# A fused two-block kernel: 32-row tap tables, a new order at the start of the second block, and a gated delta rule with its side products and norm re-cut

## The chip, the cores and the metric

One core of one Trainium2 chip runs the whole program. The metric is device time of one execution in microseconds (us). TensorE (PE), VectorE (DVE), ScalarE (ACT), GpSimd (POOL) and SyncE (SP) each have their own queue of instructions and wait for each other by semaphores; in this kernel SP issues nearly all loads.

## What is computed

256 tokens of width 1024, batch 1, all in float32. A first block of one layer, then a second block of two layers:

```python
def hybrid_mixer(xn, ...):
    b_gate, c_gate, h_conv, qkv, z, beta_logit, a_logit = split(xn @ w_in)
    y_conv = b_gate * causal_depthwise_conv(c_gate * h_conv, conv_w)      # 3 taps
    q, k, v = split(silu(causal_depthwise_conv(qkv, dn_conv_w)))          # 4 heads of 128
    o = chunk_gated_delta_rule(l2norm(q), l2norm(k), v, g, beta)          # chunks of 64
    y_dn = rms_norm(o, dn_norm) * silu(z)
    return concat([y_conv, y_dn]) @ w_out
def chunk_gated_delta_rule(...):
    t_mat = inverse(1 + strict_lower(k_beta k^T * decay))                 # per chunk
    u, w = t_mat @ v_beta, t_mat @ (k_beta * exp(g))
    intra = (q k^T) * decay
    for each chunk:                                                       # the scan
        v_new = u - w @ state
        o = (q * exp(g)) @ state + intra @ v_new
        state = state * exp(g_last) + k_dec^T @ v_new
first block:  h += hybrid_mixer;  h += cross_attention(mem);  h += peer_ffn;  x = rms_norm(h)
second block: x += gate * conv_mixer(x)   # 31-tap depthwise convolution, layer norm
              x += gate * pool_mixer(x)   # window means of 2, 4, 8, 16
```

`peer_ffn` takes the 16 best of 16384 experts for each of 8 heads of each token.

## The kernel before

Activations lie transposed: channels on the partitions, 256 tokens along the free dimension. Weights come as tiles of 128x1024 float32 (512 KB), each loaded by SP into a buffer `raw` (L113). ACT rounds a tile to the matmul's fp32r format (`hi`, L142), DVE (POOL for some) subtracts (`lo`, L144), and PE runs 24 matmuls of 128x256 on it: `hi` with the upper part of the activation, `hi` with its lower part, `lo` with the upper part (L155 to L157, L186 to L188, L1263 to L1265). Before the tiles in `plan` come in one fixed order, through rings of three buffers, so a load starts when a buffer comes free and a tile is split when its turn comes.

All other work is written as generators (`spawn`), which `tick` moves on between the tiles: evacuations of PSUM, convolutions, norms, the chain of the delta rule. Each engine's queue is then ordered by the framework's own timeline scheduler, within the priorities that the code gives (`urgent`, `high_priority`, `issue_after`). An engine runs its queue strictly in order.

The places that the change touches:

- **The mixer (L496 to L531).** In this order: the projections of k, two of four blocks of the attention's memory values (`values(0, 1)`), q, v, `values(2, 3)`, z, four pairs of `ch_evac` (convolution branch, `cp` and `ycv`, L693 to L698), two pairs of the b gate (`b_evac`, L703); then `residual` with `w_out`, whose matmuls L186 to L188 read the mixer's output `xb`: `b_evac` writes its first half (L289 and L297 split it), the delta rule its second.
- **The delta rule (`delta`, L737 to L927).** Per block of 128 tokens (two), it builds the chunk inverse by five levels of small f32 matmuls (L790, L797, L802), one step per tick. After all levels come `kbg` and `kdec` (L822, L824), and then, when q and v are there, `vb` (L833), `w`, `u`, the masked product `it` (L849) and two zero-padded copies of decayed q (`qd`, L855; POOL clears their other halves). The scan has four chunk steps: `pws` (L877), `E` = u minus it (L878, the new values), `pd` (L884), the state `S` (L891 for each head; L887 in the first). The output `po` (L900, L902) is copied by ACT. At the end the norm runs per pair of heads over all tokens: square `sqo` (L910), `on` (L912), `ov` (L914), Ln, Exp, one Newton step (L244 to L246), a POOL multiply by silu(z), then L926 and the split L289, L290.
- **Loads for the second block (`second_prep`, L1331 to L1365).** During the second half of `peer_down` (L1236 to L1266) a generator has SP load `rcnt`, `fwd`, the tap tables `ftap` (31x512) and `dw` (31x1024), and later `inv`, between the weight tiles.
- **The start of the second block (`second`, L1396).** `first_out` (L1287) makes the last sums `s` (L1298). From `s` follow `v` (L1408), `rho` (L1410, L1411, Newton) and the input `xah`, `xal` (`mod_input`, L1386, L1387) for the first matmul `mmv` (L212). The taps' transform is eight matmuls of `dw` and `ftap` (`wfm`, `wfp`, L1422) with a copy each on ACT (L1423), and `x0_gen` takes a column sum `cs` (L268) and rescales `h`.

Of the kernel before, what the change touches and what calls it, by code (L numbers as in the profile page):

```python
# [6 lines left out]
F32 = mybir.dt.float32  # L7
# [33 lines left out]
class Net:  # L41
# [26 lines left out]
    def plan(self):  # L68
# [428 lines left out]
    def mixer(self):  # L497
# [29 lines left out]
        for p in range(2):  # L527
            b = self.pair(xa, lambda ps, p=p: self.b_evac(ps, p))
# [207 lines left out]

    def delta(self):  # L737
# [69 lines left out]
        up_y(0)  # L807
        yield
        for li in range(1, nl):
            up_te(0, li)  # L810
            up_y(1)
            yield
            if li < nl - 1:
                up_y(0)
            up_te(1, li)
            yield
        for tb in range(2):
# [6 lines left out]
            V.tensor_mul(kdec[tb], pk, bc(self.ed[:, tb, :]))  # L824
            yield
        yield from self.wait("q0", "q1", "v0", "v1")
        us, wTs, inT, qds = [], [], [], []
        for tb in range(2):
            pv = pst("pv")
            for hh in R4:  # L830
                P.transpose(pv[:, hh, :], vT[:, hh, TS[tb]], ident)
            vb = t512(f"am{tb}")
            V.tensor_mul(vb, pv, bc(self.beta[:, tb, :]))  # L833
# [12 lines left out]
            for hh in R4:
                P.matmul(pq[:, hh, :], lhsT=kT[:, hh, TS[tb]], rhs=qT[:, hh, TS[tb]], start=True, stop=True)
            it = t512(f"A{tb}")
            V.tensor_mul(it, pq, self.decT[tb])  # L849
            qd = []  # L850
            for c in range(2):
                x = t512(f"kbg{tb}" if c else f"dA{tb}")
                G.memset(x[:, :, 64 * (1 - c):64 * (2 - c)], 0.0)
# [961 lines left out]
```

## Time and profile before

| what | value |
|---|---|
| median of 3 runs | 1341.28 us (1340.36 to 1341.85) |
| the profiled execution | 1340.44 us |
| its span in the trace | 1338.2 us |
| mean granted clock of TensorE | 0.987 of full speed |
| busy: PE, DVE, ACT, POOL | 1291.0, 988.9, 643.1, 168.0 us |
| loads | 236.88 MB, 178 GB/s over the span |

The span is the part of the execution that the trace covers; 2.2 us lie around it. PE is busy for 96% of the span, so 47 us of the span are left in which it does nothing, and a granted clock under 1 tells that part of its busy time ran at the lower of two levels.

### The profile page before, as it was taken

The numbers are of one execution on the slowest core, as the hardware profiler recorded it, in microseconds if no ns is written. First come the engines' busy times: TensorE is split into PE (matmuls) and PEld (weight loads), VectorE is DVE, ScalarE is ACT, GpSimd is POOL, SyncE is SP. The second block draws the span as 40 slices with busy tenths as digits, with TensorE's granted clock in tenths as the row PEclk, the third lists the DMA queues.
The fourth block names the chain that finished last, engine by engine and source line by source line (L and its number), as shares of the span: only waits on it lengthen the run. The fifth ranks groups of instructions, "written<-read, shape, count | busy, mean of one in ns | idle before, by whom it ended". The sixth has DMA issues, their size and how long they took to land.

```text
span 1338.2 us, 27259 instructions
## 1 busy us (share of the span) xinstructions
PE 1291.0 (96%) x11212; PEld 1262.5 (94%) x11212; DVE 988.9 (74%) x1885; ACT 643.1 (48%) x841; POOL 168.0 (13%) x175
## 2 busy tenths in 40 slices
PE   7999988999999999999999999998999998998988
PEld 7999978989999999999999999997999996998987
DVE  7897756458488837888878999985666666677884
ACT  6674335445554544343444344444444445356652
POOL 0000000002728362000000000010100000000000
PEclk9999998999999999999999999998999998998999
DMA  7644324434566667666677766676777772433553
GB/s 241 198 143 139 90 85 136 147 116 153 174 190 179 198 181 231 214 204 212 200 222 214 215 199 210 205 238 184 234 235 236 235 221 71 137 120 103 183 166 107
DMA packets 67340, 239.69 MB, mean 179 GB/s; under 512 B 8146, under 2 KB 8402, under 8 KB 67088
## 3 DMA queue, kind: packets, MB, share of 16 engines
q1 hardware_dynamic: 59536, 212.79, 52.7%
q0 software_dynamic: 7680, 25.17, 5.7%
q8 instruction: 87, 1.43, 0.4%
q14 instruction: 37, 0.30, 0.1%
HBM read 236.88 MB, written 1.05 MB: 178 GB/s over the span
## 4 chain that ended last, share of the span: by engine, by line
PE 90%; DVE 4%; ACT 2%; DMA 2%; issue 1%; SPq 0%; DVEq 0%; ACTq 0%
PE mm L155 14%; PE mm L157 14%; PE mm L156 14%; PE y L1263 9%; PE y L1265 9%; PE y L1264 9%; DVE lo L144 2%; PE mmv L212 2%; PE mm L187 2%; PE mmv L214 2%; PE mmv L213 2%; PE mm L188 2%; PE mm L186 2%; PE G L1215 1%; PE G L1216 1%; DMA raw<-in_V 1%
## 5 line engine op out<-in xcount | busy, mean ns | idle before, releaser
L142 ACT ACTIVATE hi<-raw 128x1024 fp32r<-128x1024 f32 x391 | 412.7, 1060 | 554.8 <-PE mm L156 229.0
L144 DVE TENSOR_TENSOR lo<-raw,hi 128x1024 fp32r<-128x1024 f32 x347 | 423.8, 1224 | 184.0 <-ACT hi L142 182.8
L155 PE MATMUL mm<-xbh,hi 128*128 128x256 f32 x1128 | 319.4, 283 | 0.3 <-ACT hi L142 0.3
L157 PE MATMUL mm<-xbh,lo 128*128 128x256 f32 x1128 | 316.8, 281 | 1.0 <-DVE lo L144 0.8
L156 PE MATMUL mm<-xbl,hi 128*128 128x256 f32 x1128 | 316.1, 280 | 0.0
L1263 PE MATMUL y<-xbh,hi 128*128 128x256 f32 x1008 | 285.1, 283 | 5.0 <-ACT hi L142 5.0
L1264 PE MATMUL y<-xbl,hi 128*128 128x256 f32 x1008 | 284.3, 282 | 0.0
L1265 PE MATMUL y<-xbh,lo 128*128 128x256 f32 x1008 | 283.8, 282 | 0.5 <-DVE lo L144 0.5
L157 PEld LDWEIGHTS mm<-xbh,lo 128*128 128x128 f32 x1128 | 212.2, 188 | 1.6 <-DVE lo L144 1.6
L155 PEld LDWEIGHTS mm<-xbh,hi 128*128 128x128 f32 x1128 | 212.6, 188 | 0.6 <-ACT hi L142 0.5
L156 PEld LDWEIGHTS mm<-xbl,hi 128*128 128x128 f32 x1128 | 212.6, 189 | 0.1
L1263 PEld LDWEIGHTS y<-xbh,hi 128*128 128x128 f32 x1008 | 190.9, 190 | 5.2 <-ACT hi L142 5.2
L1265 PEld LDWEIGHTS y<-xbh,lo 128*128 128x128 f32 x1008 | 190.6, 189 | 1.5 <-DVE xbl L297 0.8
L1264 PEld LDWEIGHTS y<-xbl,hi 128*128 128x128 f32 x1008 | 191.2, 190 | 0.0
L155 PE MATMUL mm<-xah,hi 128*128 128x256 f32 x448 | 128.2, 287 | 3.1 <-ACT xah L1386 3.1
L144 POOL TENSOR_TENSOR lo<-raw,hi 128x1024 fp32r<-128x1024 f32 x44 | 106.1, 2413 | 199.4 <-DVE mt L1094 123.5
L156 PE MATMUL mm<-xal,hi 128*128 128x256 f32 x448 | 128.5, 287 | 0.7 <-DVE xal L1387 0.7
L157 PE MATMUL mm<-xah,lo 128*128 128x256 f32 x448 | 128.2, 287 | 0.5 <-DVE lo L144 0.5
L1323 POOL DMA_DIRECT2D wm<-in_w_mod x96 | 51.7, 539 | 528.2 <-DVE wm L1326 512.3
L155 PEld LDWEIGHTS mm<-xah,hi 128*128 128x128 f32 x448 | 84.9, 190 | 4.3 <-ACT xah L1386 3.3
L1326 DVE SCALAR_TENSOR_TENSOR wm<-wm,silu_c 128x512 f32<-128x512 f32 x96 | 68.9, 718 | 25.0 <-DMA wm<-in_w_mod 24.6
L156 PEld LDWEIGHTS mm<-xal,hi 128*128 128x128 f32 x448 | 85.0, 190 | 2.0 <-DVE xal L1387 0.9
(463 smaller groups left out, 2181.1 us busy)
## 6 DMA issues: line engine op xcount, KB each, us to landing
raw<-in_U SPq DMA_DIRECT2D x128, 512.0 KB, 3.7
raw<-in_V SPq DMA_DIRECT2D x128, 512.0 KB, 4.2
wm<-in_w_mod POOLq DMA_DIRECT2D x96, 256.0 KB, 4.0
raw<-in_w_in SPq DMA_DIRECT2D x28, 512.0 KB, 3.7
raw<-in_cv_ab SPq DMA_DIRECT2D x16, 512.0 KB, 3.7
raw<-in_pl_in SPq DMA_DIRECT2D x16, 512.0 KB, 4.0
raw<-in_w_xk SPq DMA_DIRECT2D x8, 512.0 KB, 4.8
raw<-in_w_xv SPq DMA_DIRECT2D x8, 512.0 KB, 4.2
```

Of the source, the lines that this page charges most:

```text
L142: self.A.activation(hi, raw, AF.Copy)
L144: i = (self.G if self.order[m][1] else self.V).tensor_sub(lo, raw, hi.bitcast(F32))
L155: self.P.matmul(ps, lhsT=hi[:, w], rhs=xh[:, k, :], start=(k == 0 and first), stop=False, skip_group_check=True)
L156: self.P.matmul(ps, lhsT=hi[:, w], rhs=xl[:, k, :], start=False, stop=False, skip_group_check=True)
L157: self.last_mm = self.P.matmul(ps, lhsT=lo[:, w], rhs=xh[:, k, :], start=False, stop=(k == KB - 1), skip_group_check=True)
L186: self.P.matmul(o, lhsT=hi[:, c], rhs=xh[:, k, :], start=a, stop=False, skip_group_check=True)
L187: self.P.matmul(o, lhsT=hi[:, c], rhs=xl[:, k, :], start=False, stop=False, skip_group_check=True)
L1263: P.matmul(o, lhsT=hi[:, w], rhs=wh[:, s, :], start=(j == 0 and db % 2 == 0), stop=False, skip_group_check=True)
L1264: P.matmul(o, lhsT=hi[:, w], rhs=wl[:, s, :], start=False, stop=False, skip_group_check=True)
L1265: P.matmul(o, lhsT=lo[:, w], rhs=wh[:, s, :], start=False, stop=(j == 127), skip_group_check=True)
L1323: nc.gpsimd.dma_start(w, self.I["w_mod"][n, :, 512 * c:512 * (c + 1)])
L1326: V.scalar_tensor_tensor(w, w, 1.0, s, op0=OP.mult, op1=OP.mult, accum_out=part[:, n, c:c + 1])
```

## The change

Three parts. (1) `ftap` and `dw` get 32 rows, the last of zeros. (2) At the start of the second block the chain to `rho` and `mod_input` has high priority, the taps' matmuls after the first two wait for the last `s`, their copies for the Exp of `rho`, and the rescaling of `h` for the end of `mod_input`. (3) In the mixer all four `values` stand behind k. `keys` (for `kbg`, `kdec`) runs inside levels 2 and 3; a new generator `sides` makes `vb`, `it` and `qd` when the levels are done, beside `delta`; `qd` is no longer padded, its matmuls cover 64 columns. The norm runs per block of 128 tokens (`norm`), squares straight from PSUM, and takes silu(z) and the gain in one DVE operation. The last two pairs of tiles (the b gate) are not started until the scan has been issued, and stand behind the last `po` on PE.

```diff
 CW = 31
+CP = 32
...
-        add([I["w_xv"][b] for b in range(4)], "V")
-        add([w[b] for b in (*range(12, 16), *range(20, 24))], "V")
-        add([I["w_xv"][b] for b in range(4, 8)], "V")
-        add([w[b] for b in range(24, 28)], "V")
+        add([I["w_xv"][b] for b in range(8)], "V")
+        add([w[b] for b in (*range(12, 16), *range(20, 28))], "V")
...
-                self.values(0, 1)
+                self.values(0, 1, 2, 3)
             if nm == "q":
                 self.spawn(self.qsum())
-        self.values(2, 3)
+            if nm == "v":
+                self.spawn(self.urgent(self.sides()))
...
-        for p in range(2):
-            b = self.pair(xa, lambda ps, p=p: self.b_evac(ps, p))
+        while "scan" not in self.flags:
+            self.tick()
+        with self.tc.issue_after(self.last_po.ins):
+            for p in range(2):
+                b = self.pair(xa, lambda ps, p=p: self.b_evac(ps, p))
...
+    def sides(self):
...
+        yield from self.wait("v0", "v1", "levels")
+        self.vb = []
...
+            pv = self.psT.tile([128, 4, 128], F32, tag="t", name="pv")
+            for hh in range(4):
+                P.transpose(pv[:, hh, :], vT[:, hh, ts], self.ident)
+            vb = mix.tile([128, 4, 128], F32, tag="S", bufs=2, name="vb")
+            V.tensor_mul(vb, pv, self.beta[:, tb, :].unsqueeze(2).to_broadcast([128, 4, 128]))
+            self.vb.append(vb)
+        self.flags.add("vb")
...
+            pq = self.psT.tile([128, 4, 128], F32, tag="t", name="pq")
...
+            it = mix.tile([128, 4, 128], F32, tag=f"A{tb}", name="it")
+            V.tensor_mul(it, pq, self.decT[tb])
+            qd = mix.tile([128, 4, 128], F32, tag=f"dA{tb}", name="qd")
+            V.tensor_mul(qd, qT[:, :, ts], self.egr[tb])
+            self.inT.append(it)
+            self.qd.append(qd)
+        self.flags.add("it")
...
+        up_y(0)
+        yield
+        for li in range(1, nl):
+            up_te(0, li)
+            up_y(1)
+            if li in (2, 3):
+                keys(li - 2)
+            yield
+            if li < nl - 1:
+                up_y(0)
+            up_te(1, li)
+            yield
+        self.flags.add("levels")
...
+        yield from self.wait("vb")
...
+        yield from self.wait("it", "z0", "z1", "qv")
...
+        def norm(tb, po):
+            o, v, r, q = oT[:, :, TS[tb]], t512(f"yy{tb}"), t512(f"T{tb}"), t512(f"am{tb}")
+            A.activation(q, po, AF.Square)
+            V.scalar_tensor_tensor(o, po, self.col("dn_norm", 0), self.zs[:, :, TS[tb]], op0=OP.mult, op1=OP.mult)
+            yield
+            ps = pst("on")
+            P.matmul(ps, lhsT=self.ones, rhs=q, start=True, stop=True)
+            V.scalar_tensor_tensor(v, ps, 1.0 / 128, self.qv[:, :, TS[tb]], op0=OP.mult, op1=OP.add)
+            A.activation(r, v, AF.Ln)
...
+            V.tensor_mul(o, o, r)
+            V.scalar_tensor_tensor(q, q, -1.0, v, op0=OP.mult, op1=OP.mult)
+            V.scalar_tensor_tensor(o, q, 1.5, o, op0=OP.add, op1=OP.mult)
...
+            x = [t[:, 4:8, TS[tb]] for t in self.xb]
+            A.activation(x[0], o, AF.Copy)
+            V.tensor_sub(x[1], o, x[0].bitcast(F32))
...
-                yield
...
-                if c == 0:
-                    yield
...
-                        P.matmul(po[:, hh, :], lhsT=before[c][:, hh, :], rhs=qds[tb][c][:, hh, :], start=first, stop=False)
+                        cs = slice(64 * c, 64 * c + 64)
+                        P.matmul(po[:, hh, cs], lhsT=before[c][:, hh, :], rhs=self.qd[tb][:, hh, cs], start=first,
+                                 stop=False, skip_group_check=True)
                         first = False
-                P.matmul(po[:, hh, :], lhsT=vn[:, hh, :], rhs=inT[tb][:, hh, :], start=first, stop=True)
-            A.activation(oT[:, :, TS[tb]], po, AF.Copy)
-            yield
...
-            G.tensor_mul(o, o, self.zs[:, 2 * p:2 * p + 2, :])
...
+                self.last_po = P.matmul(po[:, hh, :], lhsT=vn[:, hh, :], rhs=self.inT[tb][:, hh, :], start=first,
+                                        stop=True, skip_group_check=True)
+            n = norm(tb, po)
+            next(n)
+            if tb == 0:
+                n0 = n
+            else:
+                for _ in n0:
+                    pass
+                for _ in n:
+                    pass
+                self.flags.add("scan")
...
-        self.ftap = pool.tile([CW, 4, 128], F32, name="ftap")
+        self.ftap = pool.tile([CP, 4, 128], F32, name="ftap")
         nc.sync.dma_start(self.ftap, I["ftap"])
-        self.dw = pool.tile([CW, D], F32, name="dw")
...
-        V.tensor_scalar(v2, s2, EPS * EPS, None, op0=OP.add)
         rho = post.tile([128, T], F32, name="rho")
-        A.activation(rho, v2, AF.Ln)
-        A.activation(rho, rho, AF.Exp, scale=-0.5)
-        self.rsqrt2(post, v2, rho)
-        done = self.mod_input(0, xa, rho)
+        with self.tc.high_priority():
+            V.tensor_scalar(v2, s2, EPS * EPS, None, op0=OP.add)
+            A.activation(rho, v2, AF.Ln)
+            made = A.activation(rho, rho, AF.Exp, scale=-0.5)
+            self.rsqrt2(post, v2, rho)
+            done = self.mod_input(0, xa, rho)
...
-                P.matmul(ps, lhsT=self.ftap[:, m, :], rhs=self.dw[:, c * 512:(c + 1) * 512], start=True, stop=True)
-                A.activation(wf[m // 2][:, m % 2, c * 512:(c + 1) * 512], ps, AF.Copy)
+                with self.tc.issue_after(self.last_s.ins) if m else nullcontext():
+                    P.matmul(ps, lhsT=self.ftap[:, m, :], rhs=self.dw[:, c * 512:(c + 1) * 512], start=True, stop=True)
+                with self.tc.issue_after(made.ins) if m else nullcontext():
+                    A.activation(wf[m // 2][:, m % 2, c * 512:(c + 1) * 512], ps, AF.Copy)
...
-            self.rsqrt2(post, v1, r1)
...
-                V.scalar_tensor_tensor(h[:, k, :], h[:, k, :], self.col("norm_final", k), r1, op0=OP.mult, op1=OP.mult)
+                with self.tc.issue_after(done.ins):
+                    V.scalar_tensor_tensor(h[:, k, :], h[:, k, :], self.col("norm_final", k), r1, op0=OP.mult, op1=OP.mult)
```

What the scheduler makes of it is read from the order of the instructions. On PE, at the start of the second block, stood (`s` are the sums, `cs` the column sum, `mmv` the first projection):

```order
L1422 MATMUL wfm<-dw,ftap 128x512
L1298 MATMUL s_13884<-sq_13886,gf_12129 128x256 x2
L1298 MATMUL s_13884<-sq_13903,gf_12129 128x256 x2
L1422 MATMUL wfp<-dw,ftap 128x512 x4
L1298 MATMUL s_13884<-sq_13922,gf_12129 128x256 x2
L1298 MATMUL s_13884<-sq_13940,gf_12129 128x256 x2
L1422 MATMUL wfp<-dw,ftap 128x512
L268 MATMUL cs<-acc_13907,ones 128x256 x2
L1422 MATMUL wfp<-dw,ftap 128x512
L212 MATMUL mmv<-hi,xah 128x256
```

And now:

```order
L1447 MATMUL wfm<-dw,ftap 128x512
L1321 MATMUL s_13872<-sq_13874,gf_12117 128x256 x2
L1321 MATMUL s_13872<-sq_13891,gf_12117 128x256 x2
L1321 MATMUL s_13872<-sq_13910,gf_12117 128x256 x2
L1321 MATMUL s_13872<-sq_13928,gf_12117 128x256 x2
L1447 MATMUL wfp<-dw,ftap 128x512 x4
L267 MATMUL cs<-acc_13895,ones 128x256 x2
L1447 MATMUL wfp<-dw,ftap 128x512 x2
L211 MATMUL mmv<-hi,xah 128x256
```

All four rows of `s` have moved ahead of `wfp`. On PE at the end of the mixer stood (last `po`, `on` of the norm, first matmuls of `w_out`):

```order
L902 MATMUL po<-A_1541,E_1585 128x128
L900 MATMUL po<-dA_1543,S 128x128
L900 MATMUL po<-kbg_1546,S 128x128
L902 MATMUL po<-A_1541,E_1585 128x128
L912 MATMUL on<-sqo,ones 128x512 x2
L186 MATMUL mm<-xbh,hi 128x256 x2
L187 MATMUL mm<-xbl,hi 128x256
```

Now the last `po` is followed by matmuls of the b gate (its four tiles are 96 matmuls):

```order
L939 MATMUL po<-it,E_1842 128x128
L936 MATMUL po<-qd,S 128x64 x2
L939 MATMUL po<-it,E_1842 128x128
L154 MATMUL mm<-xah,hi 128x256
L155 MATMUL mm<-xal,hi 128x256
L156 MATMUL mm<-xah,lo 128x256
```

And these are the first rows of `w_out` now:

```order
L154 MATMUL mm<-xah,hi 128x256
L155 MATMUL mm<-xal,hi 128x256
L156 MATMUL mm<-xah,lo 128x256
L185 MATMUL mm<-xbh,hi 128x256 x2
L186 MATMUL mm<-xbl,hi 128x256
L187 MATMUL mm<-xbh,lo 128x256
```

All tiles of the mixer stood ahead of the last `pd`; four now stand between the last `po` and `w_out`, with `on` of the second block of tokens among them. On DVE stood, in the scan from its second `E` on (`lo` belongs to tiles, L703 and L297 to the b gate, L914 and L244 to L246 to the norm):

```order
L878 TENSOR_TENSOR E_1550<-T_1500,pws 64x512
L703 TENSOR_TENSOR ycv<-ycv,mm 128x512
L144 TENSOR_TENSOR lo<-raw,hi 128x1024
L297 TENSOR_TENSOR xbl<-ycv,xbh 128x512
L891 SCALAR_TENSOR_TENSOR S<-S,egr,pd 128x128 x4
L144 TENSOR_TENSOR lo<-raw,hi 128x1024
L878 TENSOR_TENSOR E_1585<-T_1534,pws 64x512
L703 TENSOR_TENSOR ycv<-ycv,mm 128x512
L891 SCALAR_TENSOR_TENSOR S<-S,egr,pd 128x128 x4
L144 TENSOR_TENSOR lo<-raw,hi 128x1024
L297 TENSOR_TENSOR xbl<-ycv,xbh 128x512
L878 TENSOR_TENSOR E_1585<-T_1534,pws 64x512
```

Now it reads, from the scan's first state on (`cp`, `ycv` belong to the convolution, L886 and L890 to the norm):

```order
L924 COPY S<-pd 128x512
L916 TENSOR_TENSOR E_1803<-T_1671,pws 64x512
L143 TENSOR_TENSOR lo<-raw,hi 128x1024
L697 TENSOR_TENSOR cp<-cp,mm 128x256
L928 SCALAR_TENSOR_TENSOR S<-S,egr,pd 128x128 x4
L700 TENSOR_SCALAR ycv<-cp,cols 128x256
L702 SCALAR_TENSOR_TENSOR ycv<-cp,cols,ycv 128x256 x2
L886 SCALAR_TENSOR_TENSOR oT<-po,cols,zs 128x4x128
L916 TENSOR_TENSOR E_1842<-T_1678,pws 64x512
L928 SCALAR_TENSOR_TENSOR S<-S,egr,pd 128x128 x4
L890 SCALAR_TENSOR_TENSOR yy_1837<-on,qv 128x512
L916 TENSOR_TENSOR E_1842<-T_1678,pws 64x512
```

In place of b-gate products, the convolution and the first norm stand between the scan's `S` and `E`.

## Rows read from the trace of the kernel before

A row of a window gives the stretch, its length, then for PE, PEld, DVE, ACT and POOL the busy us and the number of instructions, then PE's granted clock, the share of the DMA engines' time that was busy, and GB/s. In a timeline, "x8" counts records: an f32 matmul leaves two. "[1.84 <-ACT xah L1386]" is idle time before a row and what ended it.

**Rows 1.** The page's first part: busy time, share, instructions by engine.
```profile
PE 1291.0 (96%) x11212; PEld 1262.5 (94%) x11212; DVE 988.9 (74%) x1885; ACT 643.1 (48%) x841; POOL 168.0 (13%) x175
```

**Rows 2.** Waits of PE, whole span: total us, times, longest.
```profile
PE mm L186 <- ACT xbh L289: 5.6, 2, 5.0
PE y L1263 <- ACT hi L142: 5.0, 1, 5.0
...
PE po L902 <- DVE E L878: 1.6, 1, 1.6
```

**Rows 3.** Windows in the second half of `peer_down`.
```profile
896.00:904.00 8.00, 8.00 (x71) 8.00 (x69) 5.34 (x7) 3.59 (x4) 0.76 (x2) 1.00 0.96 323
...
910.00:913.00 3.00, 0.00 (x0) 0.00 (x0) 0.00 (x0) 0.29 (x1) 0.00 (x0) 1.00 0.06 26
913.80:920.30 6.50, 6.01 (x26) 5.72 (x27) 4.98 (x7) 5.47 (x7) 0.07 (x1) 0.50 0.28 90
```

**Rows 4.** Timeline of SP's queue there: start, us, instruction.
```profile
895.12 0.75 SPq L1341 DMA_DIRECT2D fwd<-in_fwd  x1
...
896.29 0.26 SPq L1346 DMA_DIRECT2D dw<-in_cv_dw  x1
```

**Rows 5.** DMA issues, whole span: KB each, median us to landing.
```profile
raw<-in_V SPq DMA_DIRECT2D x128, 512.0 KB, 4.2
...
fwd<-in_fwd SPq DMA_DIRECT2D x1, 512.0 KB, 6.1
...
dw<-in_cv_dw SPq DMA_DIRECT2D x1, 124.0 KB
```

**Rows 6.** Chain of waits, 893 to 916 us: start us, us, what.
```profile
897.33 15.28 DMA raw<-in_V
...
912.71 1.06 ACT hi L142
```

**Rows 7.** Timeline of PE, start of the second block: start, us, instruction, [idle].
```profile
1107.45 3.70 PE L1422 MATMUL wfp<-dw,ftap 31*128 31x512 f32 x8
1111.08 3.48 PE L1298 MATMUL s<-sq,gf 128*128 128x256 f32 x8
...
1115.69 1.13 PE L268 MATMUL cs<-acc,ones 128*128 128x256 f32 x4
...
1119.71 0.58 PE L212 MATMUL mmv<-hi,xah 128*128 128x256 f32 x1 [1.84 <-ACT xah L1386]
```

**Rows 8.** Timeline of DVE at the same place.
```profile
1114.60 0.42 DVE L1408 TENSOR_SCALAR v<-s 128x256 f32<-128x256 f32 x1 [5.59 <-PE s L1298]
```

**Rows 9.** Windows at the start of the second block.
```profile
1107.50:1111.40 3.90, 3.90 (x10) 1.65 (x10) 1.41 (x3) 2.63 (x5) 0.00 (x0) 1.00 0.80 260
1111.40:1114.90 3.50, 3.50 (x9) 2.40 (x8) 0.30 (x1) 0.39 (x1) 0.00 (x0) 0.51 0.01 5
...
1118.20:1125.10 6.90, 5.39 (x24) 5.25 (x25) 6.53 (x17) 3.44 (x9) 0.00 (x0) 0.51 0.00 0
```

**Rows 10.** Windows at the end of the mixer, and one in attention.
```profile
187.50:203.40 15.90, 7.53 (x48) 5.51 (x47) 9.14 (x16) 6.36 (x10) 2.49 (x2) 1.00 0.21 67
203.40:210.30 6.90, 6.38 (x27) 5.87 (x28) 3.24 (x5) 0.63 (x1) 0.00 (x0) 0.51 0.22 75
...
260.00:290.00 30.00, 26.50 (x176) 23.48 (x176) 11.55 (x24) 13.32 (x28) 0.00 (x0) 1.00 0.21 61
```

**Rows 11.** DVE by line, 150 to 212 us: busy us, mean ns, idle.
```profile
L144 DVE TENSOR_TENSOR lo<-raw,hi 128x1024 fp32r<-128x1024 f32 x9 | 11.0, 1223 | 10.6 <-ACT hi L142 10.6
L698 DVE SCALAR_TENSOR_TENSOR ycv<-cp,cols,ycv 128x256 f32<-128x256 f32 x6 | 2.9, 480 | 0.1
L891 DVE SCALAR_TENSOR_TENSOR S<-S,egr,pd 128x128 f32<-128x128 f32 x8 | 2.2, 344 | 0.5 <-PE pd L884 0.4
L878 DVE TENSOR_TENSOR E<-T,pws 64x512 f32<-64x512 f32 x3 | 2.1, 685 | 0.1
```

**Rows 12.** Window in the mixer's inverse levels.
```profile
102.00:153.00 51.00, 51.00 (x447) 51.00 (x446) 34.86 (x53) 21.79 (x32) 0.30 (x3) 1.00 0.37 106
```

More of the change, by code (lines that the diff above doesn't have):

```diff
@@ L735, in wait @@
             yield "wait"
+    def sides(self):
+        mix, V, P = self.mix, self.V, self.P
+        kT, qT, vT = (self.qkvT[c] for c in "kqv")
+        yield from self.wait("v0", "v1", "levels")
+        self.vb = []
+        for tb in range(2):
+            ts = slice(tb * 128, (tb + 1) * 128)
+            pv = self.psT.tile([128, 4, 128], F32, tag="t", name="pv")
[5 more added lines that the diff above has]
+        self.flags.add("vb")
+        yield from self.wait("q0", "q1")
+        self.inT, self.qd = [], []
+        for tb in range(2):
+            ts = slice(tb * 128, (tb + 1) * 128)
+            pq = self.psT.tile([128, 4, 128], F32, tag="t", name="pq")
+            for hh in range(4):
+                P.matmul(pq[:, hh, :], lhsT=kT[:, hh, ts], rhs=qT[:, hh, ts], start=True, stop=True)
+            it = mix.tile([128, 4, 128], F32, tag=f"A{tb}", name="it")
[5 more added lines that the diff above has]
+        self.flags.add("it")
     def delta(self):
@@ L805, in up_te, with keys @@
                 V.tensor_mul(am[tb], As[tb], lev(li + 1))
-        up_y(0)
-        yield
-        for li in range(1, nl):
-            up_te(0, li)
-            up_y(1)
-            yield
-            if li < nl - 1:
-                up_y(0)
-            up_te(1, li)
-            yield
-        for tb in range(2):
+        def keys(tb):
             pk = pst("pk")
@@ L824, in delta @@
             V.tensor_mul(kdec[tb], pk, bc(self.ed[:, tb, :]))
-            yield
-        yield from self.wait("q0", "q1", "v0", "v1")
-        us, wTs, inT, qds = [], [], [], []
-        for tb in range(2):
[L829 to L833, printed above, removed]
+        up_y(0)
[5 more added lines that the diff above has]
+                keys(li - 2)
+            yield
+            if li < nl - 1:
[3 more added lines that the diff above has]
+        self.flags.add("levels")
+        ws, us = [], []
+        for tb in range(2):
             pw = pst("pw")
@@ L838, in delta @@
             A.activation(w, pw, AF.Copy)
-            yield
+            ws.append(w)
+        yield from self.wait("vb")
+        for tb in range(2):
             pu = pst("pu")
             for hh in R4:
-                P.matmul(pu[:, hh, :], lhsT=Es[tb][:, hh, :], rhs=vb[:, hh, :], start=True, stop=True)
+                P.matmul(pu[:, hh, :], lhsT=Es[tb][:, hh, :], rhs=self.vb[tb][:, hh, :], start=True, stop=True)
             u = t512(f"T{tb}")
             A.activation(u, pu, AF.Copy)
-            pq = pst("pq")
@@ L846, in delta @@
[L846 to L853, printed above, removed]
-                lo = 64 * c
-                V.tensor_mul(x[:, :, lo:lo + 64], qT[:, :, tb * 128 + lo:tb * 128 + lo + 64],
-                             self.egr[tb][:, :, lo:lo + 64])
-                qd.append(x)
@@ L866, in delta @@
+        S = first = None
         for tb in range(2):
@@ L876, in delta @@
                     for hh in R4:
-                        P.matmul(pw[:, hh, :], lhsT=wTs[tb][:, hh, :], rhs=S[:, hh, :], start=True, stop=True)
+                        P.matmul(pw[:, hh, :], lhsT=ws[tb][:, hh, :], rhs=S[:, hh, :], start=True, stop=True)
                     V.tensor_sub(vn[rows], us[tb][rows], pw[rows])
-                yield
                 if tb == 1 and c == 1:
@@ L892, in delta @@
                 S = Sn
-                if c == 0:
-                    yield
             po = pst("po")
@@ L1297, in first_out @@
             k = 2 * p + i
-            P.matmul(self.s2, lhsT=self.gf2[:, k, :], rhs=sq[:, i, :], start=(k == 0), stop=(k == KB - 1))
+            self.last_s = P.matmul(self.s2, lhsT=self.gf2[:, k, :], rhs=sq[:, i, :], start=(k == 0), stop=(k == KB - 1))
         if p == 0:
```

45 lines of the change are left out of this document (11 added, 34 removed).

## Prediction

> **What bounds the kernel now.** I read the page's first part, then the waits of PE, then windows around each wait that the change touches. PE is busy 1291.0 of 1338.2 us [rows 1], so no edit off PE's path can gain anything by itself: a gain must come out of the 47 us in which PE stands, or out of its busy time at the lower clock. The waits list shows where it stands [rows 2]: one wait of 5.0 us for `hi` in the second `peer_down`, one of 5.0 us for `xbh` at the end of the mixer, one of 1.6 us for `E` in the scan; at the start of the second block the timeline adds 1.84 us in front of `mmv` [rows 7]. Behind three of these places a window shows a granted clock of 0.50 or 0.51 [rows 3, 9, 10], so PE runs at 1.2 in place of 2.4 GHz there, and half of its busy time in such a window is loss too. These three places are the three parts of the change.
>
> **32-row tables.** In `peer_down` the loads are nearly at their limit from 896 to 904 us: share 0.96, 323 GB/s. From 910 to 913 us, while PE stands, the share is 0.06, which is one engine of 16, and that one moves 26 GB/s [rows 3]. `dw` and `ftap`, with 124 and 62 KB, were issued at 896.3 and just before, ahead of the `raw` of 897.33 [rows 4, 5], and this `raw` took 15.28 us where 4.2 is the median [rows 5, 6]. At 26 GB/s the 186 KB take 7.2 us. So I read it thus: the 31-row tables go through one engine, and the share that this engine has of the tile behind them comes last. The Trainium skill states such a rule in "DMA: Bandwidth & Descriptors", section "Why a DMA increments its semaphore by 16 and not by 1": a load issued by SP uses the largest number of engines up to 16 that divides the outermost dimension, so one for 31 rows and 16 for 32. The trace agrees for 31 (0.06 is 1/16); no row shows a load of 32 rows.
>
> With the tables spread, `fwd`, issued at 895.12 with 6.1 us to landing [rows 4, 5], lands at 901.2; the tables and the tile, 190 and 512 KB, take 2.2 us more at 323 GB/s, so 903.4; `hi` 1.06 [rows 6] and `lo` 1.22 [rows 11] end at 905.7. PE runs out at 908.8 (913.8 less its wait of 5.0), so 3 us are spare. The gain is the wait of 5.0, then half of the 6.01 busy at clock 0.50, 3.0, and the 0.5 in which PE idles inside that window [rows 3]: 8.5. I leave 0.5 for `ih`, which waits in ACT's queue for `inv`, loaded right behind. **−8.0**; bounds 0, when the sum of the loads and not the tables is what is late, and −8.5. A loss is excluded: the zero row adds 6 KB, and PE's time goes by columns (the `wfp` rows have 512).
>
> **Start of the second block.** Before, 8 records of `wfp` (3.70 us) stand between the halves of `s`, whose second half then runs for 3.48 at clock 0.51; `v` follows at 1114.60, and `mmv` 5.1 later at 1119.71 [rows 7 to 9]. The last `s` needs no `wfp`: by the 1107.45 at which the first half ends plus 8 records at the full clock (half of 3.48) it can end at 1109.2. The vector chain of 5.1 gives `mmv` at 1114.3. But PE must first run 12 records of `wfp` (3.70 × 12/8 = 5.5) and `cs` (1.0, its start to the next row's), which gives 1115.7: PE is later and counts. That is 4.0 earlier than 1119.71. The copies of `wfp`, now behind the Exp, are off this path: they feed the convolution's products, a group of tiles later.
>
> What the clock does is open. After 1118.2 PE loses 2.7 (half of 5.39 busy at 0.51), and before it 1.7 in `s` [rows 9]. If it stays up throughout, the gain is 4.0 + 2.7 = 6.7. If it falls behind `wfp` as it did in these rows, although PE was busy 3.90 of 3.90 us in the window ahead, the last 6 us up to `mmv` stretch by about 2.8, and 1.2 is left. I take **−3.0**, nearer to the lower end, because that fall stands behind a stretch of `wfp` in the row. By the Trainium skill, "TensorE: Matmul & The Clock Gate", section "What's actually happening", the clock follows how busy PE has been, and a PE without a gap would keep it: the sum would be −6.7. The row disagrees, with no idle ahead of the fall; this is the first rival below.
>
> **Values behind k, side products out of the chain.** PE has the same tiles to run. The ten level steps move beside other tiles. In the window of the levels PE is full, 51.00 of 51.00, and DVE has 34.86 [rows 12]. In the new order DVE has some 80 instructions between the first transposes and the end of the levels, 14 of them `lo` at 1.22 and 20 convolution steps at 0.48, about 56 us in all at the means of their kinds, against about 62 us of PE. That still fits, but a step can come late: **+0.5**, bounds 0 and +3. The side products and keys cost DVE the same; POOL loses four clears and two products that nobody on the path waits for after the last `po`, except in the norm.
>
> **End of the mixer.** From 187.5 to 203.4 us PE is busy 7.53 of 15.9, so it stands 8.4; then 6.38 busy run at 0.51, which costs 3.2, and 0.5 idle [rows 10]: 12.1 in all. The change puts 96 matmuls (10.8 us by the 71 in 8.00 us of [rows 3]) behind the last `po`, over the norm. In exchange the scan runs bare, and its waits come back: with `S` at 4 × 0.344, `E` at 0.69, `lo` at 1.22 and the three convolution operations at up to 0.48 [rows 11] ahead of them in DVE's queue, I get idle times of 0.9 (first `pws` to `pd`), 0.5 (`S` behind `lo` and `cp`), 1.7 (`E` behind `ycv` and the norm's first product; [rows 2] has 1.6 for a bare `E`), 0.2 and 0.9: 4.2. At the end, `xbh` of the b gate waits for its own tiles, which are now last: a product and a copy of about 0.7 each, like `E`, with a `hi` of 1.06 and a `lo` of 1.22 ahead of them on their engines, 3.7, of which I let 0.4 overlap: 3.3. So 7.5 replaces 12.1: **−4.6**. Bounds: −9 if the norm and the b gate's split are wholly hidden and only the scan's shorter waits remain; +1 if two waits like the 5.0 of [rows 2] stand beside a half clock. The 64-column `po` matmuls save less than 1.3 and I take nothing.
>
> **Sum.** −8.0 − 3.0 + 0.5 − 4.6 = −15.1, from the profiled execution's 1340.44 to 1325.3. The median of the runs is 0.84 above that execution, so **1326** us. A change of 0.2%, 2.7 us, is about what a measurement of this kernel tells from none.
>
> **Rivals.**
> 1. The clock stays up in the second block (for it: no idle is left there; against it: [rows 9]). 3.7 better: 1322.4, and 1318 if the mixer also reaches its better bound (4.4 more). Chance 0.17.
> 2. The tables are not what was late, or 32 rows still go through one engine: the 8.0 stays. For it: 0.96 of the DMA time was in use before the gap [rows 3]; against it: the 0.06 afterwards. 1334. Chance 0.12.
> 3. The bare scan, with short matmuls and gaps, loses the clock, and the held tiles start at 1.2 GHz: 3.2 as in [rows 10], so 1329. Against it: the attention window with 3.5 idle in 30 keeps 1.00 [rows 10]. Chance 0.08.
> 4. Slower: DVE becomes the bound in the ten level steps, since values and q now evacuate beside them, and each step of the inverse comes late with no tile matmul ready in front of it. It decides from 1.6 us a step (15.6 over ten); at 2.0 it gives 1326 + 19.5 = 1345.6. Against it: 6 us spare over the stretch. Chance 0.03.
> 5. Hardly an effect, because each gap reappears a few tiles later: 1341. Chance 0.03.
>
> **How the numbers follow.** The forecast, 1321.5 to 1331, has 0.57. The range goes from 1318 (rival 1 with the mixer's bound) to 1334 (rival 2); outside it are rivals 4 and 5 and the outer ends of the others, some 0.15. Faster are the forecast and rivals 1 to 3: 0.94; the same 0.03; slower 0.03.
>
> **What would show it.** Right: no wait of `y` for `hi` near 909 us, the `raw` behind `dw` landing within some 6 us, and clock 1.00 there; `mmv` 4 us or more closer to the end of `peer_down`; no wait of 5 us before L185, but waits of `pws` and `pd` in the scan, and PE full at the levels. Wrong: a share of 0.06 again; a clock of 0.5 behind `wfp` longer than 3.5 us; PE idle in the level steps for `E` or `T`.

## The result and the profile after

| what | before | after |
|---|---|---|
| median | 1340.82 us (1339.3 to 1341.85, 4 runs) | 1323.1 us (1319.95 to 1326.81, 4 runs) |
| ratio | | 0.987, 95% interval 0.9854 to 0.9887 |
| profiled execution | 1340.44 us, span 1338.2, clock 0.987 | 1324.46 us, span 1322.7, clock 0.991 |

The change makes the kernel faster by 1.3%, and the time lies inside the forecast's range. The profiled execution, 1324.46, is 0.8 us under the 1325.3 that was added up for it; the median of the runs is 2.9 under the 1326 forecast for it. The runs after are spread wider than those before, and their time follows the mean clock: 1319.95 at 0.995, 1321.74 at 0.993, 1324.46 at 0.991, 1326.81 at 0.989.

Three marks cut the profiled executions into the three parts of the change: the issue of `fwd` (895.12 before [rows 4], 890.77 after), the `wfm` ahead of the last sums, and the end of the span. Before, in the timeline of PE (start, us, instruction), the second mark is

```profile
1104.48 1.12 PE L1422 MATMUL wfm<-dw,ftap 31*128 31x512 f32 x2
```

and after, in the timelines of SP and of PE:

```profile
890.77 0.59 SPq L1364 DMA_DIRECT2D fwd<-in_fwd  x1
...
891.88 0.42 SPq L1369 DMA_DIRECT2D dw<-in_cv_dw  x1
```

```profile
1091.88 1.12 PE L1447 MATMUL wfm<-dw,ftap 32*128 32x512 f32 x2
1092.93 3.89 PE L1321 MATMUL s<-sq,gf 128*128 128x256 f32 x16
1096.75 4.14 PE L1447 MATMUL wfp<-dw,ftap 32*128 32x512 f32 x8
1100.83 2.07 PE L267 MATMUL cs<-acc,ones 128*128 128x256 f32 x4
1102.83 3.78 PE L1447 MATMUL wfp<-dw,ftap 32*128 32x512 f32 x4
1106.54 0.58 PE L211 MATMUL mmv<-hi,xah 128*128 128x256 f32 x1
```

| stretch | before | after | difference | forecast |
|---|---|---|---|---|
| start to `fwd`: the mixer | 895.12 | 890.77 | -4.35 | -4.6 + 0.5 = -4.1 |
| `fwd` to `wfm`: the tables | 1104.48 - 895.12 = 209.36 | 1091.88 - 890.77 = 201.11 | -8.25 | -8.0 |
| `wfm` to the end: the second block | 1338.2 - 1104.48 = 233.72 | 1322.7 - 1091.88 = 230.82 | -2.90 | -3.0 |
| sum | | | -15.50 | -15.1 |

The first row leans on one execution of the kernel before. E1 and E2 below, which have the old mixer too, issue `fwd` at 894.17 and 894.16; against them the mixer's part is -3.4.

Where it came from: the page's first part, PE's waits over the whole span (total us, times, longest), DMA issues (KB, median us to landing) and windows (stretch, length, busy us of PE, PEld, DVE, ACT, POOL, then the granted clock, DMA share, GB/s) of the changed kernel.

```profile
PE 1287.2 (97%) x11212; PEld 1259.3 (95%) x11212; DVE 988.8 (75%) x1883; ACT 642.6 (49%) x841; POOL 164.5 (12%) x169
```

```profile
PE mm L154 <- ACT hi L141: 8.0, 2, 7.7
...
PE pd L921 <- DVE E L916: 2.1, 2, 1.2
...
PE mm L185 <- ACT xbh L899: 1.5, 1, 1.5
...
PE po L939 <- DVE E L916: 0.8, 1, 0.8
PE mm L186 <- DVE xbl L900: 0.8, 1, 0.8
...
PE pws L915 <- DVE S L928: 0.4, 1, 0.4
```

```profile
dw<-in_cv_dw SPq DMA_DIRECT2D x1, 128.0 KB, 7.4
```

```profile
891.00:899.00 8.00, 8.00 (x71) 8.00 (x70) 3.95 (x5) 2.58 (x4) 1.42 (x2) 1.00 0.92 282
899.00:905.00 6.00, 6.00 (x51) 5.80 (x51) 4.95 (x7) 4.11 (x6) 0.54 (x1) 1.00 0.81 256
905.00:911.00 6.00, 6.00 (x45) 5.11 (x44) 4.29 (x6) 4.29 (x5) 0.54 (x1) 1.00 0.71 227
...
180.00:184.00 4.00, 2.83 (x17) 2.16 (x18) 2.44 (x6) 1.02 (x2) 0.00 (x0) 1.00 0.00 0
...
188.00:196.00 8.00, 8.00 (x65) 7.52 (x64) 4.99 (x7) 4.88 (x7) 0.00 (x0) 1.00 0.27 70
...
202.00:206.00 4.00, 4.00 (x23) 4.00 (x23) 0.00 (x0) 0.39 (x2) 0.00 (x0) 0.57 0.62 245
...
1099.90:1106.50 6.60, 6.60 (x10) 2.33 (x8) 2.48 (x7) 3.48 (x8) 0.00 (x0) 0.50 0.00 0
1106.50:1110.50 4.00, 4.00 (x21) 3.96 (x21) 3.16 (x8) 3.02 (x7) 0.00 (x0) 0.55 0.00 0
```

PE's busy time fell by 3.8 us against [rows 1]; the other 11.7 of the 15.5 are idle time. The wait of 5.0 us of `y` [rows 2] is gone, `dw` lands in 7.4 us, and PE is full at clock 1.00 from 891 to 911 us, where [rows 3] had a hole and a clock of 0.50. The wait of 5.0 before `w_out` became 1.5 and 0.8, the scan has 2.1, 0.8 and 0.4 in its place. And the clock is still lost behind `w_out`'s waits (0.57 from 202 to 206) and under the taps: 0.50 from 1099.9 to 1106.5, with PE busy 6.60 of 6.60. With the 0.55 of the next 4 us that makes some 10 us at the lower level, in one piece; before the change it was two pieces of 3.5 and 6.9 us [rows 9].

### The profile page after: what moved, and what is told of

Same layout as the page of the kernel before. It is cut to its first block, busy times and chain, and to the rows that moved or that the text cites. A ratio compares the mean times of both kernels' runs of the same rounds, so it can differ in the third digit from the quotient of the medians.

```text
span 1322.7 us, 27240 instructions
## 1 busy us (share of the span) xinstructions
PE 1287.2 (97%) x11212; PEld 1259.3 (95%) x11212; DVE 988.8 (75%) x1883; ACT 642.6 (49%) x841; POOL 164.5 (12%) x169
## 4 chain that ended last, share of the span: by engine, by line
PE 93%; DVE 3%; ACT 2%; DMA 1%; issue 1%; SPq 0%; DVEq 0%; ACTq 0%
PE mm L156 14%; PE mm L154 14%; PE mm L155 14%; PE y L1286 9%; PE y L1287 9%; PE y L1288 9%; PE mmv L211 2%; PE mmv L212 2%; PE mmv L213 2%; PE mm L186 2%; PE mm L187 2%; PE mm L185 2%; DVE lo L143 1%; PE G L1238 1%; PE G L1239 1%; ACT hi L141 1%
```

## Experiments

All ratios are to the kernel before, run on the same chip in the same batch; E1 to E4, E5 to E8 and E9 to E12 are one batch each.

**E1: the tables alone.** Kernel before with both tables padded by a row of zeros:

```diff
+CP = 32
...
-        self.ftap = pool.tile([CW, 4, 128], F32, name="ftap")
+        self.ftap = pool.tile([CP, 4, 128], F32, name="ftap")
...
-        self.dw = pool.tile([CW, D], F32, name="dw")
+        self.dw = pool.tile([CP, D], F32, name="dw")
```

> The kernel before with 32-row tables alone. Theory (31 rows go through one DMA engine, 32 through all): 8.3 us faster than before, no wait of y for hi near 909 us, no stretch with a DMA share of 0.06, clock 1.00 there. Rival (the volume of rcnt, fwd and inv is late): within 1 us of before, the wait stays near 5 us.

Ratio 0.9936 (0.9923 to 0.9948), 8.6 us. No wait of `y` is left between 880 and 960 us. A window behind the table loads:

```profile
909.00:915.00 6.00, 6.00 (x45) 5.11 (x44) 4.22 (x7) 4.01 (x5) 0.54 (x1) 1.00 0.69 236
```

PE is full, the clock 1.00, no stretch has a share of 0.06, and from `fwd` to `wfm` 1095.25 - 894.17 = 201.1, as in the changed kernel. The theory held: the added row of zeros is the whole of this part, and since it adds bytes, the volume of the loads was not what was late.

**E2: the order in the second block alone.** Kernel before with the high priority, the two `issue_after` of the taps and that of `h`.

```diff
+        with self.tc.high_priority():
...
+                with self.tc.issue_after(self.last_s.ins) if m else nullcontext():
...
+                with self.tc.issue_after(made.ins) if m else nullcontext():
```

> The kernel before with the new order at the start of the second block alone. Theory (PE's queue is the bound there, and the clock falls behind the tap matmuls): mmv 1 us closer to the end of peer_down than before, 1 to 4 us faster in all, clock 0.50 in the tap matmuls. Rival (the clock stays at the upper level, and the run with half a clock was an exception): 6 to 7 us faster, clock 1.00 up to mmv.

Ratio 0.9963 (0.9949 to 0.9977), 5.0 us, runs from 1331.21 to 1338.33. In the profiled execution (the shortest) `wfm` starts at 1103.27 and `mmv` at 1114.74: 11.47, with clock 1.00. The mean lies between theory (1 to 4) and rival (6 to 7); the profiled execution is as the rival has it. E4 shows that one program can have either outcome.

**E3: the mixer alone.** Kernel before with the changes to `plan`, `mixer`, `sides` and `delta`.

```diff
-                self.values(0, 1)
+                self.values(0, 1, 2, 3)
...
+        with self.tc.issue_after(self.last_po.ins):
```

> The kernel before with the mixer's part alone. Theory (the three parts are independent): 4.3 us faster than before, and the three single gains add up to that of the change within 2 us. Rival (the parts share a gain, since an earlier mixer shifts the loads or the clock later on): the sum of the three is off by more than 3 us.

Ratio 0.996 (0.9946 to 0.9974), 5.4 us; median 1333.12, but 12 runs from 1331.73 to 1340.27, nine of them within 1331.7 to 1336. The three parts alone give 8.6 + 5.0 + 5.4 = 19.0 us, the whole 17.4 in the same batch (E4's ratio): they add up within 2 us, as the theory has it. Each single gain is uncertain by nearly 2 us, though, and that of the whole by over 3, so a shared gain of a few us would not show.

**E4 and E9: the changed kernel again.** No edit.

> The changed kernel once more, without an edit. Its four runs lay between 1319.95 and 1326.81 us with mean clocks of 0.995 to 0.989. Theory (one place, the start of the second block, loses the clock in some executions and keeps it in others): again a spread of some 5 us, 1.1 us for each 0.001 of clock, and where the profiled run is a short one its trace has clock 1.00 from the last s to mmv. Rival (several places vary a little each): the second block's start looks the same in a short run as in a long one.

> The changed kernel a third time, as the measure beside the three that follow. Theory (two places lose the clock in some executions, the bare scan at 180 to 196 us and the taps at 1100 to 1110 us): median 0.986 to 0.988 of before, a spread of over 5 us, runs from 1317 to 1328. Rival (only one place varies): executions fall into two groups, some 5 us apart.

E4: 0.987 (0.9845 to 0.9895), 6 runs from 1317.5 (clock 0.996) to 1328.82 (0.989). E9: 0.9851 (0.9836 to 0.9867), 5 runs from 1318.1 (0.996) to 1323.93 (0.990). The profiled execution of E4, a run of middle length, kept the clock. Timeline of its PE at the start of the second block:

```profile
1093.98 1.12 PE L1447 MATMUL wfm<-dw,ftap 32*128 32x512 f32 x2
1095.03 3.90 PE L1321 MATMUL s<-sq,gf 128*128 128x256 f32 x16
1098.86 3.69 PE L1447 MATMUL wfp<-dw,ftap 32*128 32x512 f32 x8
1102.48 1.13 PE L267 MATMUL cs<-acc,ones 128*128 128x256 f32 x4
1103.55 1.98 PE L1447 MATMUL wfp<-dw,ftap 32*128 32x512 f32 x4
1105.45 0.39 PE L211 MATMUL mmv<-hi,xah 128*128 128x256 f32 x1
```

From `wfm` to `mmv` it takes 11.47 where the first one took 1106.54 - 1091.88 = 14.66: the same program and order, with `wfp` at 3.69 and 1.98 in place of 4.14 and 3.78. The profiled execution of E9 lost the clock there (14.92), and for a short stretch in the scan (0.57 from 180 to 184 us). So the second block's start takes one of two values by execution, some 3 us apart up to `mmv`. This is the theory of E4, but not the whole of the spread, which was 11 us where 5 were expected: the clock of the scan varies too, as the theory of E9 has it and E7 confirms. Two groups of times 5 us apart, the rival of E9, are not seen: the 15 runs of the changed kernel fill the range from 1317.5 to 1328.82 in steps of at most 2.0.

**E5: no hold.** The changed kernel with

```diff
-        while "scan" not in self.flags:
-            self.tick()
-        with self.tc.issue_after(self.last_po.ins):
-            for p in range(2):
-                b = self.pair(xa, lambda ps, p=p: self.b_evac(ps, p))
+        for p in range(2):
+            b = self.pair(xa, lambda ps, p=p: self.b_evac(ps, p))
```

> The changed kernel with the last four tiles of the mixer not held back: the host loop that waits for the scan and the order behind the last po are taken out, all else stays. Theory (the hold is what hides the norm, and the rest of the mixer's part mainly prepares it): PE stands some 5 us before the first matmul of w_out again and loses the clock behind it, 3 to 5 us slower than the changed kernel. Rival (the shorter chain does it: side products out of it and a norm by tokens): within 1 us of the changed kernel.

Ratio 0.9867 (0.9852 to 0.9882), 1321.49 to 1323.08: that is the rival's value, as if the hold were worth nothing in the mean. The changed kernel was not run in this batch; its ratios in the three others are 0.987, 0.987 and 0.9851, so a difference of two or three us would not show. The mechanism of the theory is there all the same. PE's waits from 150 to 215 us:

```profile
PE mm L185 <- ACT xbh L895: 4.9, 1, 4.9
PE po L935 <- DVE E L912: 2.1, 1, 2.1
PE on L885 <- ACT am L881: 0.8, 1, 0.8
```

The wait of 4.9 before `w_out` is back, and `fwd` is issued at 892.32, 1.6 later than the 890.77 of the changed kernel. The hold can lose this again in some executions: E7 shows a place.

**E6: the hold alone.** Kernel before with the host loop and the `issue_after` of the change; the flag "scan" is set when the old `delta` ends.

```diff
+        while "scan" not in self.flags:
+            self.tick()
+        with self.tc.issue_after(self.last_po.ins):
```

> The kernel before with the hold of the last four tiles alone (the host waits until the old delta generator has ended, the b gate stands behind the last po on PE); side products, padded qd and the norm by head pairs stay. Theory (the hold alone has most of the gain): 2 to 4 us faster than before. Rival (the old chain is too long to stand bare: w, u, it and qd are made in it after q and v, so the scan's steps stand without tiles for longer than the norm hidden): 0 to 5 us slower than before.

Ratio 0.9993 (0.9984 to 1.0002): no gain, between theory and rival. PE's waits at the end of its mixer in the profiled execution, the shortest of 11:

```profile
PE mm L186 <- ACT xbh L289: 2.8, 2, 1.5
PE mm L187 <- DVE xbl L290: 1.9, 2, 1.7
```

Here, with clock 1.00 from 163 to 210 us, the hold pays: `fwd` is issued at 891.94, 3.2 before the 895.12 of [rows 4] and 2.2 before E1 and E2. `w_out` waits 2.8 and 1.9 in four pieces, little less than the 5.0 of [rows 2]; what pays is above all the clock, which had fallen behind this wait [rows 10] and now stays up. Ten of the eleven runs, though, have a mean clock of 0.984 to 0.988 where this one has 0.991. This execution also shows the second block's old order without a fall of the clock at the taps:

```profile
1103.58 1.12 PE L1426 MATMUL wfm<-dw,ftap 31*128 31x512 f32 x2
1104.63 1.99 PE L1302 MATMUL s<-sq,gf 128*128 128x256 f32 x8
1106.55 3.69 PE L1426 MATMUL wfp<-dw,ftap 31*128 31x512 f32 x8
1110.18 1.99 PE L1302 MATMUL s<-sq,gf 128*128 128x256 f32 x8
...
1117.17 0.39 PE L212 MATMUL mmv<-hi,xah 128*128 128x256 f32 x1 [1.84 <-ACT xah L1390]
```

From `wfm` to `mmv` 1117.17 - 1103.58 = 13.59, against 11.47 in the new order with the clock up (E2, E4).

**E7: taps on 128 rows.** The changed kernel with

```diff
-        self.ftap = pool.tile([CP, 4, 128], F32, name="ftap")
-        nc.sync.dma_start(self.ftap, I["ftap"])
-        self.dw = pool.tile([CP, D], F32, name="dw")
-        nc.sync.dma_start(self.dw, I["cv_dw"])
+        self.ftap = pool.tile([128, 4, 128], F32, name="ftap")
+        self.dw = pool.tile([128, D], F32, name="dw")
+        for a, b in ((32, 64), (64, 128)):
+            G.memset(self.ftap[a:b], 0.0)
+            G.memset(self.dw[a:b], 0.0)
+        nc.sync.dma_start(self.ftap[0:CP], I["ftap"])
+        nc.sync.dma_start(self.dw[0:CP], I["cv_dw"])
```

> The changed kernel with the taps' matmuls on 128 rows: the tables lie in tiles of 128 rows, rows 32 to 127 set to zero by POOL beside peer_down, and the loads stay those of 32 rows. Theory (matmuls that use 32 of 128 rows are what lets the clock fall in some executions): clock 1.00 from the last s to mmv in the profile, and all runs at the short end, 1317 to 1320 us on the chip of the first batch. Rival A (long matmuls with little weight loading let it fall): as the changed kernel, a spread of 5 us or more. Rival B (the clears on POOL delay the loads of the tables): the wait for hi near 905 us comes back.

Ratio 0.984 (0.982 to 0.986), runs 1315.21, 1317.64, 1320.33, 1321.95 and 1324.32; four of the five have a clock of 0.995 or 0.996. The clock at the taps is as the theory has it; the runs are not all at the short end, and the interval overlaps those of the changed kernel. The profiled execution is the 1324.32. The start of its second block keeps the clock:

```profile
1098.07 1.02 PE L1450 MATMUL wfm<-dw,ftap 128*128 128x512 f32 x2
...
1102.74 3.60 PE L1450 MATMUL wfp<-dw,ftap 128*128 128x512 f32 x8
...
1107.04 1.88 PE L1450 MATMUL wfp<-dw,ftap 128*128 128x512 f32 x4
1108.35 0.68 PE L211 MATMUL mmv<-hi,xah 128*128 128x256 f32 x1
```

The wait of rival B is not there. The spread of 9 us is as rival A has it, but not for its reason, as the scan below shows. From `wfm` to `mmv` it takes 10.28, less than in any execution with 32 rows: besides the clock, PE is quicker between these matmuls and those of 128 rows around them. What made this execution long is the scan:

```profile
168.00:180.00 12.00, 9.86 (x78) 8.94 (x76) 7.70 (x15) 2.60 (x4) 0.00 (x0) 1.00 0.32 95
180.00:196.00 16.00, 14.84 (x64) 13.04 (x65) 6.02 (x12) 4.06 (x6) 0.00 (x0) 0.57 0.00 0
```

From 180 to 196 us PE ran at 0.57, and `fwd` was issued at 896.78, 6.0 later than in the changed kernel's first execution, with the same order on PE. This is the third rival, in an execution of a kernel whose mixer is that of the change.

**E8: taps in 256 columns.** The changed kernel with

```diff
-                    P.matmul(ps, lhsT=self.ftap[:, m, :], rhs=self.dw[:, c * 512:(c + 1) * 512], start=True, stop=True)
+                    for q in range(2):
+                        P.matmul(ps[:, 256 * q:256 * q + 256], lhsT=self.ftap[:, m, :],
+                                 rhs=self.dw[:, c * 512 + 256 * q:c * 512 + 256 * q + 256], start=True, stop=True)
```

> The changed kernel with each matmul of the taps cut in two of 256 columns, 32 rows as before. Rival A of the run with 128 rows (long matmuls with little weight loading let the clock fall) expects clock 1.00 from the last s to mmv and runs at the short end, 1317 to 1320; the theory of rows expects the spread of the changed kernel, and up to 1 us more for the second set of weight loads.

Ratio 0.9872 (0.9851 to 0.9893); one run of five is short (1318.35, clock 0.995), and the profiled execution loses the clock under the taps again (14.16 from `wfm` to `mmv`). Rival A is out for this execution: twice the number of weight loads did not keep the clock.

**E10: half of the hold.** The changed kernel with the first pair of the b gate ahead of the loop:

```diff
+        self.pair(xa, lambda ps: self.b_evac(ps, 0))
         while "scan" not in self.flags:
             self.tick()
         with self.tc.issue_after(self.last_po.ins):
-            for p in range(2):
-                b = self.pair(xa, lambda ps, p=p: self.b_evac(ps, p))
+            b = self.pair(xa, lambda ps: self.b_evac(ps, 1))
```

> The changed kernel with only the last two of the mixer's tiles held back: the first pair of the b gate runs as filler in the scan, the second behind the last po. Theory (the hold hides the norm at the price of a scan that can lose the clock; half the hold keeps the clock and hides most of the norm): clock 1.00 from 165 to 195 us, 1 to 3 us faster than the changed kernel in the median, and no run as long as 1328. Rival (five us of matmuls do not cover the norm): a wait of 2 us or more before the first matmul of w_out, no faster than the changed kernel.

Ratio 0.991 (0.989 to 0.993), slower than the changed kernel in the same batch (E9, 0.9851) by 0.6%, 8 us. The theory fell, and its rival came. PE's waits from 150 to 215 us:

```profile
PE mm L185 <- ACT xbh L898: 5.5, 1, 5.5
PE pd L920 <- DVE E L915: 1.0, 1, 1.0
PE pws L914 <- DVE S L927: 0.8, 1, 0.8
PE po L938 <- DVE E L915: 0.8, 1, 0.8
```

Two held tiles leave a wait of 5.5 in front of `w_out` (four left 1.5) and still leave the end of the scan bare. They pay for both. The profiled execution is 3.0 us longer than the first of the changed kernel: `fwd` comes 2.6 later, and another 1.8 are a slower pace from `fwd` to `wfm` (last section), so not all of its loss is the hold's.

**E11 and E12: taps on 128 rows with half of the hold, and with none.** The edits of E7 and E10, and of E7 and E5.

> The changed kernel with both: the taps' matmuls on 128 rows and half of the hold. Theory (each removes one of the two places that lose the clock): 3 to 6 us faster than the changed kernel in the median, 1315 to 1319, spread under 5 us. Rival (the clock falls by chance somewhere else then): as the changed kernel, within 1 us.

> The changed kernel with the taps' matmuls on 128 rows and no hold. Theory: no loss of clock in the scan, the norm bare again, 2 to 4 us faster than the changed kernel in the median and 1 to 2 slower than with half of the hold, spread under 4 us. Rival (the hold is worth more than its risk): slower than the run with half of the hold by over 3 us.

E11: 0.9874 (0.9858 to 0.9889), so 4.8 us under E10, which differs only in the taps. E12: 0.9892 (0.9875 to 0.9908), with clocks of 0.989 to 0.993. Neither beats the changed kernel, so both theories fell: against E9, in the same batch, E11 is 3 us slower and E12 5.5. Both profiled executions keep the clock under the taps. But E11 loses it in the scan, with half of the hold (0.78 and 0.80 in the two 4 us from 184 us on), so half of the hold does not keep that place safe. And E12, which has no hold, being slower than E9 goes against E5, where leaving the hold out cost nothing: what the hold is worth in the mean stays open.

Counted over the 14 profiled executions: with 31 or 32 rows the clock fell between `wfm` and `mmv` in seven of eleven (before, after, E1, E3, E8, E9, E10) and stayed up in four (E2, E4, E5, E6); with 128 rows it fell in none of three (E7, E11, E12). The two marks of all of them, in us:

| part | executions | value |
|---|---|---|
| issue of `fwd`, old mixer | before, E1, E2 | 895.12, 894.17, 894.16 |
| hold alone | E6 | 891.94 |
| re-cut, no hold | E5, E12 | 892.32, 892.44 |
| re-cut, half of the hold | E10, E11 | 893.34, 895.17 |
| re-cut and hold | after, E3, E4, E8, E9 | 890.77, 890.82, 891.06, 889.12, 890.13 |
| the same, the clock long down in the scan | E7 | 896.78 |
| `wfm` to the end, old order | before, E1, E3, E6 | 233.7, 235.0, 231.6, 231.2 |
| new order, clock lost at the taps | after, E8, E9, E10 | 230.8, 230.0, 231.3, 229.4 |
| new order, clock kept at the taps | E2, E4, E5 | 226.1, 226.5, 226.8 |
| new order, 128 rows, clock kept | E7, E11, E12 | 224.5, 223.0, 224.2 |

The second block is shorter with 128 rows than in any execution with fewer. That and E11 against E10 speak for the rows as a cause. E12 was no faster than E5, but in the profiled executions it gains 2.6 in the second block and loses 2.1 from `fwd` to `wfm` (last section), so it does not speak against. Three executions don't settle whether the clock can fall with 128 rows too, and it stays open.

## Why the prediction was right

**Tables.** Right in mechanism and size: 8.25 us by the marks where 8.0 was forecast, 8.6 alone in E1. The page "DMA: Bandwidth & Descriptors" of the Trainium skill, section "Why a DMA increments its semaphore by 16 and not by 1", has 16 engines for 32 rows; E1 agrees, with no stretch at 0.06 and no wait of `y`. The second rival is out. The `raw` behind `dw` took 8.0 us, and 7.4 in E1, where the prediction had some 6; the 3 us that it found spare covered that. Of the half microsecond kept back for `ih`, at most 0.25 shows.

**Second block.** The sum came out (-2.90 against -3.0), its parts did not, so that it fits is luck. Of "4.0 earlier than 1119.71", 1.7 was the half clock of the second `s` [rows 7, 9], not the order: with the clock up the old order takes 13.59 up to `mmv` (E6) and the new one 11.47 (E4), so the order is worth 2.1.

The two outcomes that the prediction saw are both real, and its middle value stands for neither. In the first execution the clock fell, for over 6.6 us, which was one of the prediction's signs of being wrong, and `mmv` came only 0.57 closer to `wfm` (14.66 for 15.23) where "4 us or more" was a sign of being right. For a fall it had left 1.2 and looked no further than `mmv`. But 2.33 more came behind `mmv`: the clock was back 3.6 us after `mmv`, where before the change it took 5.4 [rows 9]. By half of the difference that is worth 0.9; the rest was not traced. In E4 the clock did not fall, and from `wfm` to the end of the span it took 1320.5 - 1093.98 = 226.52, 7.2 under the 233.72 of before, where the prediction had 6.7. The first rival is thus the other of two outcomes of one program, and with a chance of 0.17 it was held too unlikely: the clock stayed up in three of the seven executions with the new order and 32 rows or fewer. Runs in which it stays up lie below the profiled one and pull the median under 1326.

The Trainium skill, "TensorE: Matmul & The Clock Gate", section "What's actually happening", lets the clock follow how busy PE has been; here it fell with PE busy in every record (6.60 of 6.60), and stayed up in another execution of the same order, so a busy PE in the trace did not decide it.

**Level steps.** The 0.5 was not there. PE is full in the stretch of [rows 12], with DVE somewhat busier (39.12 for 34.86):

```profile
102.00:153.00 51.00, 51.00 (x447) 51.00 (x447) 39.12 (x62) 23.63 (x36) 0.41 (x4) 1.00 0.33 103
```

The fourth rival did not show.

**End of the mixer.** -4.35 by the first mark, -3.4 against E1 and E2, of -4.1. The scan's waits are 2.1 + 0.8 + 0.4 = 3.3 in the list, where 4.2 was forecast; those of `w_out` 1.5 + 0.8 = 2.3, of 3.3. Not counted was the clock: 0.57 over 4.0 us behind these waits, 1.7. Together 7.3 where 7.5 was forecast, so one omission and two terms that were too long cancel. The largest wait, 1.2 before `pd`, has the cause that the order showed, in DVE's timeline after:

```profile
173.42 1.23 DVE L143 TENSOR_TENSOR lo<-raw,hi 128x1024 fp32r<-128x1024 f32 x1
...
175.02 1.11 DVE L928 SCALAR_TENSOR_TENSOR S<-S,egr,pd 128x128 f32<-128x128 f32 x4
176.05 0.35 DVE L700 TENSOR_SCALAR ycv<-cp,cols 128x256 f32<-128x256 f32 x1
176.43 1.00 DVE L702 SCALAR_TENSOR_TENSOR ycv<-cp,cols,ycv 128x256 f32<-128x256 f32 x2
177.35 0.74 DVE L886 SCALAR_TENSOR_TENSOR oT<-po,cols,zs 128x512 f32<-128x512 f32 x1
178.01 0.67 DVE L916 TENSOR_TENSOR E<-T,pws 64x512 f32<-64x512 f32 x1
```

From `S` on, the convolution's operations and the norm's product run without a gap up to `E` at 178.01. `pws` started at 176.48 and took 1.06, so `E` came 0.5 late and needed 0.67 itself: 1.2 where the forecast had 1.7 for this step.

What the prediction took for one mechanism, the hold over the norm, is by the first mark worth 1.3 to 3.3 us in five executions (889.12 to 891.06, against 892.32 and 892.44 without it) and a loss of 4.4 in E7; in the means of runs E5 has it at nothing and E12 at more. The rest of the mixer's gain is in the re-cut chain and norm, which E5 has without the hold: its wait before `w_out` is as long as before, and yet its `fwd` comes 1.8 before those of E1 and E2, 2.8 before the 895.12 of [rows 4]. Which piece of the re-cut gives how much was not tried. The third rival, at 0.08, is true of some executions: E7 lost 6 us that way, E3 (0.70 and 0.88 in the 8 us from 180 on) and E9 a little, the first one and E4 nothing.

## What to carry to other kernels

A load's row count is worth a look in the trace: a DMA share of 1/16 at the end of a burst, and a tile that lands 11 us late behind small tables, cost 8 us here, and one row of zeros in each table mended it. Where work is held back to cover a gap, count what the earlier place loses: four tiles behind the scan hid the norm and left the scan bare, two tiles did neither. And where a stretch can run at either clock, give both times and a chance for each, and follow each to the end of the stage: the middle value was right here only because the worse outcome had been priced too low.

## What the runs showed that was not expected

- The same program took 1317.5 to 1328.82 us in one batch, and the mean clock of 0.996 to 0.989 went with it. One profiled execution shows one draw; the 2.9 us of the second block could as well have been read as 7.2.
- 128 rows in place of 32 shortened `wfm` to `mmv` from 11.47 to 10.28 with the clock up in both, though the matmuls have as many columns, and no execution with 128 rows has the clock falling there.
- From `fwd` to `wfm`, with 32-row loads, it took 200.8 to 201.3 us in five profiled executions (after, E1, E5, E7, E9) and 202.6 to 202.9 in five others (E4, E8, E10, E11, E12), without a wait and at clock 1.00: 339 or 340 matmul records in 40 us in place of 343 or 344. The changed kernel itself did either (first execution and E9, E4). What slows it is not known.
